# Row sums and their spread by 32x32 block turns and one folding matmul, in an encoder layer with attention and a matrix memory

## The chip, the cores and the metric

One Trainium2 chip, one core. The time is device microseconds of one execution of the whole program; the kernel before takes 2061.98 us (median of three runs, 2061.67 to 2063.15). Lower is better. The engines are TensorE (PE, with PEld for its weight loads), VectorE (DVE), ScalarE (ACT), GpSimd (POOL) and SyncE (SP, which here issues most of the transfers).

## The reference, cut to what matters

One layer is applied to two sequences of 512 tokens with 1024 channels (`x_prompt` and `x_sample`, called 0 and 1 in the kernel), all in float32:

```python
def rms_norm(x, g):
    return x * rsqrt(mean(x * x, axis=-1) + EPS) * g

def mlstm_bidirectional(...):            # 4 heads of 128 channels
    h = h_fwd + h_bwd
    h = h * rsqrt(mean(h * h, axis=-1) + EPS)      # over a head's 128 channels
    return sigmoid(o_pre) * h * head_norm

def encoder_layer(x, ...):
    x = x + 0.5 * swiglu(rms_norm(x, ffn1_norm), ...)        # 1024 -> 2816 -> 1024
    proj = rms_norm(x, mix_norm) @ w_in
    ...                                  # att: 8 query heads, 2 key heads; mem: mlstm_bidirectional
    merged = sigmoid(g_att) * (att @ w_up_att) + sigmoid(g_mlstm) * (mem @ w_up_mlstm)
    x = x + merged @ w_out
    return x + 0.5 * swiglu(rms_norm(x, ffn2_norm), ...)     # then the final rms_norm
```

What the change touches are three of these norms: the one ahead of `w_in` ("mid norm"), the one ahead of the second feed-forward, and the one over each memory head. Each needs, for every token, the sum of squares over the channels, one over its square root, and that number multiplied into every channel.

## The kernel before, in words

**Layout.** The channels lie on the 128 partitions and the 512 tokens along the free dimension, so one tile is 128x512 and a sequence is eight such tiles. A sum over channels is therefore a sum across partitions, and the factor for a token must stand on all 128 partitions. Matmuls are done in parts: an operand is split into a high and a low part, and one product takes three matmuls of 128x128 by 128x512.

**Stages.** The first feed-forward runs over both sequences at once by a scheme of seven products (0 to 640 us of the span). Then come, for sequence 0, its projections (640 to 690), attention (690 to 840), the four memory heads (840 to 945), and the gates together with the projections of sequence 1 (945 to 1075). Sequence 1 has its attention at 1075 to 1225, its memory heads at 1225 to 1330, its merge and output until 1420. The second feed-forward fills 1420 to 2059. The two mixers are generators (`mix`) that are advanced in turns.

**The norm before.** For each tile of squares summed over the channel tiles (`accs`, `acc2`, tag `R`), `stats` takes four steps. `col_sums` turns the 128x512 tile by four TensorE transposes into PSUM (L202), so that tokens lie on partitions, and VectorE sums each 128 (L204) to a 128x4 tile: four columns of 128 tokens. `rstd_cols` computes the inverse root by a shift and three Newton rounds, twelve small VectorE operations (L161, L170, L172, three times L188, L189, L191). `bcast_psum` turns each column, spread over 128, back by four more transposes (L212), and `bcast_cols` copies PSUM to an SBUF tile with the tag `R` (L218). The 128x4 tile is kept as `r[s]` in the mid norms, where it scales values with tokens on partitions. The memory heads do the same on one tile of squares (`h2`, L1238) and let VectorE read PSUM directly when it multiplies (L1244).

**Where they stand.** There are twelve such norms: the mid norm of sequence 0 (`mid_stats(0, 100, 140)`, near 642 us), the mid norm of sequence 1 within the attention of mixer 0 (`mid_parts(1)`), the norm of sequence 0 ahead of the second feed-forward within the attention of mixer 1 (`parts2(0)`), that of sequence 1 at the second feed-forward's start (`stats2(1)`, near 1417 us), and the eight memory heads. The first norm, ahead of the first feed-forward, and the final norm do it in ways of their own and use `col_sums` and `bcast_psum` too; those calls stay.

**What sets the order.** The kernel is written in a tile framework that orders each engine's instructions by priority. Code stands in order of priority as written; `shifted(n)` moves a block later by `n` places, and `pin` keeps an instruction where the program has it. In attention, `extra` is a list of parts that are called at the third key block of heads 2, 3 and so on. Between the heads of the memory stand products of other units (`merge_att`, `out_gate`, `mem_qk`, L789) as filling. In `mem_out`, five rounds alternate four transposes of a 128x512 tile with the twelve matmuls of the head's output (L1235), and then the norm follows; the next head's `mem_head` has its score products (L1185) and their VectorE products (L1201, L1213, L1215).

**Buffers.** `T2` hands out 128x512 tiles from rings by tag: `t2` has 11 buffers, `f2` four, `R` two. PSUM has banks by pool: three for `MM`, one for `PO`, two each for `PS` and `PT`.

## Time and profile before

| | before |
|---|---|
| median of three runs | 2061.98 us (2061.67 to 2063.15) |
| span of the profiled execution | 2059.1 us |
| TensorE busy | 2047.3 us, 99%, 9445 matmuls and transposes |
| TensorE weight loads | 1691.3 us, 82% |
| VectorE busy | 1553.0 us, 75%, 2764 instructions |
| ScalarE busy | 913.0 us, 44%, 1667 instructions |
| GpSimd busy | 92.8 us, 5%, 108 instructions |
| TensorE clock | nine tenths or more in all 40 slices |
| moved to and from memory | 457.97 MB, 222 GB/s on the mean |

The profiled execution is one of its own; its span (2059.1 us) lies 2.9 us under the median of the timed runs, and the profile gives no further time for it. Rows of the profile name the line of the code (L202), the engine, the operation, the tile written and the tiles read (`pst<-ident,t`), the shape, and the count. In rows of the timeline the two numbers ahead are the start and the length in microseconds; what stands in brackets is the wait ahead of a row and what ended it. PSUM tiles are called `mm`, `pso`, `pss` and `pst` after the pools `MM`, `PO`, `PS` and `PT`.

### The profile page before, as it was taken

How to read it: one execution, taken by the hardware profiler on the slowest of the kernel's cores; microseconds unless marked ns; L12 is line 12 of the kernel's file. 1: busy time of each engine (PE TensorE's matmuls, PEld its weight loads, DVE VectorE, ACT ScalarE, POOL GpSimd, SP SyncE). 2: the span in 40 equal slices, each digit the busy share in tenths (PEclk: the TensorE clock that was granted, in tenths of full speed). 3: DMA queues.
4: the chain of work that ended last, by engine and by line, in shares of the span. 5: the costliest groups of instructions: out<-in, count | busy, mean ns of one | idle time of the engine just before them, and what ended most of it. 6: DMA issues, size and time to landing. Idle time of an engine off the chain costs nothing.

```text
span 2059.1 us, 27038 instructions
## 1 busy us (share of the span) xinstructions
PE 2047.3 (99%) x9445; PEld 1691.3 (82%) x9445; DVE 1553.0 (75%) x2764; ACT 913.0 (44%) x1667; POOL 92.8 (5%) x108
## 2 busy tenths in 40 slices
PE   9999999999999999999999999999999999999998
PEld 7888888888888888888888888888888888888887
DVE  8888889886797787675566756455788888796797
ACT  7544444442235567563334553324544444443224
POOL 0000000001003000100120000001000000000001
PEclk9999999999999999999999999999999999999999
DMA  9656556799766753877684345677656555599753
GB/s 321 198 170 221 177 191 205 243 349 348 260 227 247 223 187 130 278 259 242 197 310 160 109 140 200 196 265 239 202 175 202 194 174 184 186 342 347 276 202 119
DMA packets 311015, 457.97 MB, mean 222 GB/s; under 512 B 20232, under 2 KB 182112, under 8 KB 309600
## 3 DMA queue, kind: packets, MB, share of 16 engines
q1 hardware_dynamic: 308800, 450.27, 64.6%
q0 software_dynamic: 1920, 5.72, 0.9%
q8 instruction: 74, 1.21, 0.2%
q14 instruction: 61, 0.50, 0.1%
q10 hardware_dynamic: 160, 0.27, 0.0%
HBM read 288.25 MB, written 167.94 MB: 222 GB/s over the span
## 4 chain that ended last, share of the span: by engine, by line
PE 97%; DVE 1%; ACT 1%; DMA 1%; issue 0%; SPq 0%; ACTq 0%; DVEq 0%
PE mm L789 15%; PE pso L332 12%; PE pst L332 12%; PE mm L332 10%; PE mm L590 8%; PE pss L332 6%; PE mm L776 6%; PE pst L590 4%; PE pss L590 4%; PE mm L756 4%; PE pso L590 3%; PE pso L1066 1%; PE pss L1039 1%; PE pst L1055 1%; PE pso L1235 1%; PE pss L1185 1%
## 5 line engine op out<-in xcount | busy, mean ns | idle before, releaser
L332 PE MATMUL pst<-xc,w 128*128 128x512 f32 x1056 | 253.6, 389 | 0.0
L332 PEld LDWEIGHTS pst<-xc,w 128*128 128x128 f32 x1056 | 198.3, 188 | 41.1
L332 PE MATMUL mm<-xc,w 128*128 128x512 f32 x972 | 229.9, 390 | 0.2 <-ACT f L340 0.2
L332 PEld LDWEIGHTS mm<-xc,w 128*128 128x128 f32 x972 | 181.9, 188 | 38.1 <-ACT f L340 0.6
L590 PE MATMUL mm<-rt,w 128*128 128x512 f32 x765 | 178.9, 389 | 0.0
L789 PE MATMUL mm<-xh,w 128*128 128x512 f32 x560 | 177.6, 393 | 0.0
L590 PEld LDWEIGHTS mm<-rt,w 128*128 128x128 f32 x765 | 143.6, 188 | 29.8
L290 ACT ACTIVATE w<-t 128x512 fp32r<-128x512 f32 x176 | 106.5, 627 | 135.7 <-issue 63.1
L291 DVE TENSOR_TENSOR w<-t,w 128x512 fp32r<-128x512 f32 x176 | 117.8, 688 | 47.9 <-ACT w L290 46.6
L332 PE MATMUL pss<-xc,w 128*128 128x512 f32 x528 | 126.8, 389 | 0.0
L332 PE MATMUL pso<-xc,w 128*128 128x512 f32 x528 | 126.8, 389 | 0.0
L332 PE MATMUL pso<-xc,f 128*128 128x512 f32 x528 | 126.8, 389 | 0.0
L789 PEld LDWEIGHTS mm<-xh,w 128*128 128x128 f32 x560 | 104.7, 188 | 21.2 <-DVE w L239 0.2
L332 PEld LDWEIGHTS pss<-xc,w 128*128 128x128 f32 x528 | 99.2, 188 | 20.5
L332 PEld LDWEIGHTS pso<-xc,w 128*128 128x128 f32 x528 | 99.1, 188 | 20.5
L332 PEld LDWEIGHTS pso<-xc,f 128*128 128x128 f32 x528 | 99.1, 188 | 20.5
L776 PE MATMUL mm<-xh,w 128*128 128x512 f32 x336 | 114.5, 401 | 0.0
L789 PE MATMUL mm<-xl,w 128*128 128x512 f32 x280 | 109.7, 392 | 0.0
L673 ACT ACTIVATE w<-wr 128x512 fp32r<-128x512 f32 x72 | 45.1, 632 | 137.0 <-PE pso L590 71.4
L673 ACT ACTIVATE w<-t 128x512 fp32r<-128x512 f32 x82 | 51.8, 632 | 107.4 <-PE pst L590 62.4
L590 PE MATMUL pst<-rt,w 128*128 128x512 f32 x396 | 93.7, 389 | 0.0
L590 PE MATMUL pss<-rt,w 128*128 128x512 f32 x396 | 93.7, 389 | 0.0
(407 smaller groups left out, 4037.5 us busy)
## 6 DMA issues: line engine op xcount, KB each, us to landing
rt<-rbuf SPq DMA_DIRECT2D x154, 512.0 KB, 5.7
wpark<-w SPq DMA_DIRECT2D x104, 512.0 KB, 3.4
w<-wpark SPq DMA_DIRECT2D x104, 512.0 KB, 4.8
wr<-in_ffn_w_gate_dram SPq DMA_DIRECT2D x62, 512.0 KB, 5.3
rbuf<-tab SPq DMA_DIRECT2D x102, 256.0 KB, 3.9
wr<-in_ffn_w_up_dram SPq DMA_DIRECT2D x44, 512.0 KB, 4.5
rbuf<-f SPq DMA_DIRECT2D x72, 256.0 KB, 4.1
wr<-in_w_in_dram SPq DMA_DIRECT2D x36, 512.0 KB, 5.7
```

Source lines behind the costliest of these rows:

```text
L290: pin(nc.scalar.activation(t[:, 0], src, AF.Copy))
L291: pin(V_.tensor_tensor(t[:, 1], src, f(t[:, 0]), op=ALU.subtract))
L332: nc.tensor.matmul(p, a[:, k, :], xt[:, b, k, :], start=(first and k == 0 and i == 0), stop=(k == HK_ - 1 and i == 2), skip_group_check=True)
L590: nc.tensor.matmul(p, u[:, a, d * P:(d + 1) * P], r[:, b, ts], start=(first and q == 0 and k == 0), stop=(q == len(us) - 1 and k == 2), sk ...
L673: nc.scalar.activation(hi, src, AF.Copy)
L756: nc.tensor.matmul(p[b][:, :N], a[:, k, bs], w_[:, kl, :], start=(k == 0 and i == 0), stop=(k == KD - 1 and i == 2))
L776: pin(nc.tensor.matmul(p[0], a[:, k, :], b, start=(k == 0 and i == 0), stop=(k == n - 1 and i == 2)))
L789: nc.tensor.matmul(p, a[:, k, :], b, start=(k == 0 and i == 0), stop=(k == n - 1 and i == 2))
L1039: pin(nc.tensor.matmul(p, qT[:, h, b * P:(b + 1) * P], kv[:, hk * 2 + j, :], start=(j == 0), stop=(j == 1)))
L1055: pin(nc.tensor.transpose(p[:, b * P:(b + 1) * P], Ps[b][:, kb * P:(kb + 1) * P], ident))
L1066: pin(nc.tensor.matmul(pos[h], Vst[:, kb, h // 4, :], w, start=(kb == 0 and i == 0), stop=(kb == 3 and i == 1)))
L1185: nc.tensor.matmul(p, qk[a][:, isl], qk[b], start=(n == 0), stop=(n == 2))
```

## The change

All twelve norms get their sums and their spread in another way. The four steps become:

- `block_sums`: VectorE turns the tile of squares in blocks of 32x32 (`nc.vector.transpose`) into an `f2` tile, and sums each group of 32 along the free dimension into 16 columns of a tile `row`. Partition 32a + i then holds, in column n, the sum over the 32 channels of group a for token 32n + i.
- `block_rstd`: one TensorE matmul with the constant `fold` (128x128, 1 where the two partitions agree modulo 32) adds the four channel groups and leaves the whole sum on each of them. The twelve small VectorE operations follow, on 16 columns and in place within `row`.
- `spread_rows`: a second block turn of VectorE reads each of the 16 columns 32 times and writes the 128x512 tile of factors to SBUF (tag `R` for the norms, `f2` in the heads), where before it stood in PSUM.
- `row_cols`: for the mid norms alone, four small GpSimd copies make the 128x4 tile `r[s]` from the 16 columns.

`fold` is made by four GpSimd operations in `mix_consts`. In attention the norm is now in three parts, at heads 2, 3 and 4, instead of two, at heads 2 and 3, with the folding matmul pinned. In the memory heads `block_rstd` is shifted by 60 and the spread by 160; before, only the part from `bcast_psum` on was shifted, by 160. One other tile (`et`) shares a buffer (`fa`), and `cs` has one buffer instead of two.

```diff
-    def stats(acc):
-        return rstd_cols(col_sums(acc), 4, D)
-    def bcast_cols(r):
-        pr = bcast_psum(r)
-        R = T2(F32, "R")
-        nc.vector.tensor_copy(R, pr)
+    fold = cpool.tile([P, P], F32, name="fold")
+    def fold_const():
+        part_ = fold[:, 0:32]
+        for a in range(1, 4):
+            src = ident[:, 0:32] if a == 1 else part_
+            nc.gpsimd.tensor_tensor(part_, src, ident[:, a * 32:(a + 1) * 32], op=ALU.add)
+        nc.gpsimd.tensor_copy(fold[:, 32:P].rearrange("p (a j) -> p a j", j=32),
+                              part_.unsqueeze(1).to_broadcast([P, 3, 32]))
+    def block_sums(t, tag="f2"):
+        row = spool.tile([P, 64], F32, tag="row", bufs=1, name=nm("row"))
+        q = T2(F32, tag)
+        nc.vector.transpose(q, t)
+        nc.vector.tensor_reduce(row[:, 0:16], q.rearrange("p (n j) -> p n j", j=32), axis=AX.X, op=ALU.add)
+        return row
+    def block_rstd(row, n, keep=lambda i: i):
+        p = PT()
+        keep(nc.tensor.matmul(p[:, 0:16], fold, row[:, 0:16], start=True, stop=True))
+        V = nc.vector
+        a, y, u = [row[:, 16 * i:16 * i + 16] for i in (1, 2, 3)]
+        V.tensor_scalar(a, p[:, 0:16], 1.0 / n, EPS, op0=ALU.mult, op1=ALU.add)
...
+        return y
+    def row_stats(acc):
+        return block_rstd(block_sums(acc), D)
+    def row_cols(r16):
+        c = spool.tile([P, 4], F32, tag="rc4", bufs=2, name=nm("rc"))
+        for a in range(4):
+            ps_ = slice(a * 32, (a + 1) * 32)
+            nc.gpsimd.tensor_copy(c[ps_, :], r16[ps_, :].rearrange("p (b a) -> p a b", a=4)[:, a, :])
+        return c
+    def spread_rows(r16, R):
+        nc.vector.transpose(R.rearrange("p (n j) -> p n j", j=32), r16.unsqueeze(2).to_broadcast([P, 16, 32]))
         return R
...
-                if extra and b == 2 and h in (2, 3):
+                if extra and b == 2 and h in (2, 3, 4):
                     extra[h - 2]()
...
-            rh = rstd_cols(col_sums(h2), 4, DM)
+            row = block_sums(h2)
+            with shifted(60):
+                rh = block_rstd(row, DM)
             with shifted(160):
-                Rh = bcast_psum(rh)
+                Rh = spread_rows(rh, T2(F32, "f2"))
                 V_.scalar_tensor_tensor(og, og, hn[:, h:h + 1], Rh, op0=ALU.mult, op1=ALU.mult)
                 split(og, mem[:, h, 0, :], mem[:, h, 1, :])
...
     def mid_stats(s, a=0, b=0):
         with shifted(a):
-            r[s] = stats(accs[s])
+            r16 = row_stats(accs[s])
         with shifted(b):
-            R[s] = bcast_cols(r[s])
+            R[s] = spread_rows(r16, T2(F32, "R"))
+            r[s] = row_cols(r16)
...
     def mid_parts(s):
+        got = []
         def one():
-            r[s] = stats(accs[s])
+            got.append(block_sums(accs[s]))
         def two():
-            R[s] = bcast_cols(r[s])
-        return one, two
+            got.append(block_rstd(got[0], D, pin))
+        def three():
+            R[s] = spread_rows(got[1], T2(F32, "R"))
+            r[s] = row_cols(got[1])
+        return one, two, three
...
     def stats2(s):
-        r[s] = stats(acc2[s])
-        R2[s] = bcast_cols(r[s])
+        R2[s] = spread_rows(row_stats(acc2[s]), T2(F32, "R"))
```

`parts2` changes as `mid_parts` does, without `r[s]`. In the changed file the folding matmul is L232, the first block turn L225, its sum L226, the second block turn L258, and the lines of the memory heads lie 41 to 43 further down (L1235 is L1276, L1240 is L1281, L1185 is L1226, L1201 is L1242, and the products of L789 are L830).

TensorE at the third memory head of mixer 0, before: from the last matmuls into the head's output (L1235) over the transposes of the squares (L202) to the next head's scores (L1185), with filling (L789):

```order
L1235 MATMUL pso_7885<-t_931_7913,Vm_7266 128x512
L1235 MATMUL pso_7885<-t_933_7924,Vm_7266 128x512 x2
L1235 MATMUL pso_7885<-t_934_7925,Vm_7266 128x512
L789 MATMUL mm_8168<-att_5939,w_8060 128x512 x4
L202 MATMUL pst_7937<-ident,t_935_7934 128x128 x4
L789 MATMUL mm_8168<-att_5939,w_8060 128x512 x4
L789 MATMUL mm_8192<-att_5939,w_8060 128x512 x4
L1185 MATMUL pss_8018<-qk_7758 128x512 x3
```

The same place now, with the folding matmul (L232) in the place of the transposes:

```order
L1276 MATMUL pso_7844<-t_899_7872,Vm_7251 128x512
L1276 MATMUL pso_7844<-t_901_7883,Vm_7251 128x512 x2
L1276 MATMUL pso_7844<-t_902_7884,Vm_7251 128x512
L830 MATMUL mm_8012<-att_5934,w_7824 128x512 x2
L830 MATMUL mm_8101<-att_5934,w_8006 128x512 x12
L830 MATMUL mm_8125<-att_5934,w_8006 128x512 x2
L232 MATMUL pst_7900<-row_7896,fold 128x16
L830 MATMUL mm_8125<-att_5934,w_8006 128x512 x2
L1226 MATMUL pss_7964<-qk_7717 128x512 x3
```

Between the head's last output matmul and the first norm step on TensorE stood 4 filling matmuls; now there are 16, and the four spreading transposes (L212), which stood 15 rows further on, are gone.

VectorE at the same head, before: after the gating of the head's output (L1240), the sum of the turned squares (L204) and the small operations of the root stand among the products of the next head's scores (L1201):

```order
L1240 SCALAR_TENSOR_TENSOR box_5279<-box_5279,pso_7885 128x512
L1201 SCALAR_TENSOR_TENSOR t_951_7996,dn_7991<-pss_7992,t_951_7996 128x128
L204 TENSOR_REDUCE cs_7942<-pst_7937 128x4
L1201 SCALAR_TENSOR_TENSOR t_952_7999,dn_7991<-pss_7992,t_952_7999 128x512
L161 TENSOR_SCALAR rs_7944<-cs_7942 128x4
L1201 SCALAR_TENSOR_TENSOR t_954_8009,dn_7991<-pss_8005,t_954_8009 128x256
L170 TENSOR_SCALAR rs_7946<-rs_7944 128x4
```

And now:

```order
L1281 SCALAR_TENSOR_TENSOR box_5274<-box_5274,pso_7844 128x512
L225 STREAM_TRANSPOSE f_905_7897<-t_903_7893 128x512
L1242 SCALAR_TENSOR_TENSOR t_911_7942,dn_7937<-pss_7938,t_911_7942 128x128
L226 TENSOR_REDUCE row_7896<-f_905_7897 128x16
L1242 SCALAR_TENSOR_TENSOR t_912_7945,dn_7937<-pss_7938,t_912_7945 128x512
L1242 SCALAR_TENSOR_TENSOR t_914_7955,dn_7937<-pss_7951,t_914_7955 128x256
L1242 SCALAR_TENSOR_TENSOR t_915_7959,dn_7937<-pss_7951,t_915_7959 128x384
L1242 SCALAR_TENSOR_TENSOR t_917_7968,dn_7937<-pss_7964,t_917_7968 128x384
L235 TENSOR_SCALAR row_7896<-pst_7900 128x16
```

The block turn stands right behind the gating and ahead of the next head's products; the small operations moved behind five of those products. The spreading turn (L258) comes after the last scaling of the next head's tiles, and the multiplication with it (L1287, before L1244) two rows later.

TensorE at the start of the second feed-forward, where sequence 1's norm stands among the first products (L332), before:

```order
L332 MATMUL mm_12495<-xc_12013,w_12492 128x512 x12
L332 MATMUL mm_12555<-xc_12013,w_12547 128x512 x2
L202 MATMUL pst_12510<-ident,R_12226 128x128 x4
L332 MATMUL mm_12555<-xc_12013,w_12547 128x512 x10
L332 MATMUL mm_12495<-xc_12014,w_12492 128x512 x3
L212 MATMUL pst_12538<-ident,rs_12536 128x128 x4
L332 MATMUL mm_12495<-xc_12014,w_12492 128x512 x9
```

And now (L332 is L372):

```order
L372 MATMUL mm_12361<-xc_11879,w_12358 128x512 x12
L372 MATMUL mm_12406<-xc_11879,w_12398 128x512 x8
L232 MATMUL pst_12380<-row_12376,fold 128x16
L372 MATMUL mm_12406<-xc_11879,w_12398 128x512 x4
L372 MATMUL mm_12361<-xc_11880,w_12358 128x512 x12
```

The fold stands six products later than the transposes did, and nothing of the norm is left on TensorE behind it. Of the transfers, the first four loads from `xbuf` for the next sequence's projections (L1591) and the first four from `x2buf` (L1617) stand later in SyncE's queue than before, at place 567 instead of 544 and 717 instead of 705; both go into `f2` tiles, of which each head now takes two more.

20 lines of the change are left out of this document (15 added, 5 removed).

## Prediction

> **What bounds the kernel now.** I read the page's busy times and its chain first, then what TensorE itself waited for.
>
> ```profile
> span 2059.1 us, 27038 instructions
> PE 2047.3 (99%) x9445; PEld 1691.3 (82%) x9445; DVE 1553.0 (75%) x2764; ACT 913.0 (44%) x1667; POOL 92.8 (5%) x108
> PEclk9999999999999999999999999999999999999999
> PE 97%; DVE 1%; ACT 1%; DMA 1%; issue 0%; SPq 0%; ACTq 0%; DVEq 0%
> PE pst L987 <- DVE t L674: 0.7, 2, 0.5
> PE pst L212 <- DVE rs L191: 0.2, 1, 0.2
> ```
>
> TensorE is busy 99% of the span, at the full clock in every slice, and it carries 97% of the chain that ended last. The last two rows are from the list of TensorE's waits: between the start-up and the end it waits for almost nothing. So the end is set by how long TensorE's own instructions take in their order. A microsecond taken from that order comes off the end, as long as no other engine becomes late. VectorE, at 75%, is where the change puts its work.
>
> By stage, the table of windows has the attention of the first mixer (690 to 840), its memory heads (840 to 945), and the same two stages of the second mixer (1075 to 1225, 1225 to 1330):
>
> ```profile
> 690.00:840.00 150.00, 149.77 (x746) 122.27 (x745) 121.19 (x246) 103.26 (x205) 1.58 (x1) 1.00 0.58 190
> 840.00:945.00 105.00, 105.00 (x497) 84.78 (x496) 73.46 (x194) 54.93 (x118) 6.68 (x5) 1.00 0.78 255
> 1225.00:1330.00 105.00, 105.00 (x500) 85.66 (x499) 60.56 (x182) 40.57 (x101) 0.00 (x0) 1.00 0.57 187
> ```
>
> The columns after the length are busy time and count of PE, PEld, DVE and ACT. VectorE has 32 us of 105 free in the first memory and 44 in the second.
>
> **What leaves TensorE.** The replaced steps are four norms (two mid norms, two before the second feed-forward) and eight memory heads. Each had four transposes that turned the squares (L202) and four that spread the result (L212): 12 x 8 = 96.
>
> ```profile
> L202 PE MATMUL pst<-ident,t x32: 271/273/275, 843.1 to 1307.9; 128*128 128x128 f32 x32
> L202 PE MATMUL pst<-ident,R x20: 270/272/328, 641.5 to 2035.2; 128*128 128x128 f32 x20
> L212 PE MATMUL pst<-ident,rs x48: 270/272/323, 648.0 to 1421.5; 128*128 128x128 f32 x48
> ```
>
> Of the 20 in the second row, four belong to the final norm of the first sequence, which stays; 32 + 16 + 48 = 96. A duration of 272 ns isn't the price, since matmuls overlap. The price is read from starts, in the timeline of TensorE at the first head, against the rhythm of plain matmuls from the chain in order of time:
>
> ```profile
> 1421.81 48.30 PE mm L332 x213
> 842.18 1.07 PE L789 MATMUL mm<-att,w 128*128 128x512 f32 x4
> 843.09 0.60 PE L202 MATMUL pst<-ident,t 128*128 128x128 f32 x4
> 843.44 0.47 PE L789 MATMUL mm<-xh,w 128*128 128x512 f32 x1
> 843.76 0.39 PE L789 MATMUL mm<-xl,w 128*128 128x512 f32 x1
> ```
>
> 48.30 / 213 = 0.227 us per matmul. From the first transpose to the second matmul behind the four it is 843.76 - 843.09 = 0.67 us, of which one matmul is 0.227; the four cost 0.44, or 0.111 each. 96 x 0.111 = 10.7 us.
>
> The Trainium skill ("TensorE: Matmul & The Clock Gate", Part 4: PE-mode transpose) gives about 390 ns for a 128x128 transpose in isolation and about 275 ns in one kernel. The trace agrees with 275 as the duration of one (272), but by this sum the path holds only 0.111 of it; whoever summed durations would get 96 x 0.272 = 26.1 us, which is a rival below.
>
> **What enters TensorE.** Twelve matmuls with the 128x128 `fold` and 16 columns, in full float32. The gates already have six of that shape in each mixer:
>
> ```profile
> 680.76 0.51 PE L919 MATMUL pst<-Lt,tab 128*128 128x16 f32 x4
> 681.12 0.37 PE L919 MATMUL pst<-Lt,ones 128*128 128x16 f32 x2
> 681.35 0.60 PE L919 MATMUL pst<-Lt,tab 128*128 128x16 f32 x4
> 681.79 0.37 PE L919 MATMUL pst<-Lt,ones 128*128 128x16 f32 x2
> 682.02 0.49 PE L789 MATMUL mm<-xh,w 128*128 128x512 f32 x1
> 682.34 0.40 PE L789 MATMUL mm<-xl,w 128*128 128x512 f32 x1
> ```
>
> Six in the code are twelve in the trace, so each makes two passes. 682.34 - 680.76 - 0.227 = 1.35 us for twelve, 0.113 a pass, 0.226 a matmul: 12 x 0.226 = 2.7 us. TensorE's own balance is -10.7 + 2.7 = **-8.0 us**.
>
> **What VectorE does instead.** Per step it adds a turn of 128x512 in 32x32 blocks, a sum over 16 groups of 32, and a turn that spreads 16 columns to 512. It drops the sum of the transposed squares and, in the four norms, a copy from PSUM. The twelve little operations stay, on 16 columns instead of 4.
>
> ```profile
> L204 DVE TENSOR_REDUCE cs<-pst x13: 680/691/693, 642.6 to 2035.5; 128x4 f32<-128x512 f32 x13
> L218 DVE COPY R<-pst x4: 683/691/692, 649.2 to 1422.1; 128x512 f32<-128x512 f32 x4
> L188 DVE SCALAR_TENSOR_TENSOR rs<-rs x48: 152/163/194, 644.0 to 1420.6; 128x4 f32<-128x4 f32 x36, 128x8 f32<-128x8 f32 x6, 128x32 f32<-128x32 f32 x6
> L929 DVE TENSOR_TENSOR_SCAN f<-f x2: 402/406/411, 684.4 to 1039.9; 32x128 f32<-32x128 f32 x2
> ```
>
> The little ones hardly change: their extremes are 152 and 194 ns, with 4 and 32 columns among the forms. The sum is as long as the old one. No row shows a block turn. Its nearest is the copy of the same 128x512, 0.69 us, and I take that. A turn below it, down to half, would gain nothing, since TensorE is then simply served earlier. The upper end is VectorE's slowest kind per column, the scan: about 0.4 us for 128 columns against about 0.15 of fixed cost, so 0.25 / 128 x 512 + 0.15 = 1.2 us. Together 24 turns less 4 copies are 20 x 0.69 = 14 us in a VectorE with 500 us free over the span, and nothing on the path unless TensorE stands waiting.
>
> The Trainium skill ("VectorE: DVE Perf Modes", The three transpose paths) gives 311 ns for a block turn of 128x128 in bf16 on VectorE; no run here shows one yet, and an estimate from it lies near my 0.69. Its Rules for kernel authors send a 128x128 transpose to TensorE where PSUM will do. By that rule this change would be worth nothing; by the rows TensorE is the full engine, and the sum goes by the rows.
>
> **The new wait.** TensorE now waits at the folding matmul for the row of sums, and every matmul queued behind it waits too. The chain is read at the first head:
>
> ```profile
> 841.16 1.18 PE L1235 MATMUL pso<-t,Vm 128*128 128x512 f32 x4
> 842.38 0.60 ACT L1238 ACTIVATE t<-pso 128x512 f32<-128x512 f32 x1 [2.16 <-PE pso L1235]
> 843.01 0.69 DVE L1240 SCALAR_TENSOR_TENSOR box<-box,pso 128x512 f32<-128x512 f32 x1 [1.30 <-ACT t L1238]
> 843.61 0.68 DVE L1151 SCALAR_TENSOR_TENSOR mg<-mg,mm 128x512 f32<-128x512 f32 x1
> ```
>
> The last matmul into the head's PSUM ends at 842.34; ScalarE squares until 842.98; VectorE starts L1240 at 843.01 and can start the next thing at 843.61. Turn 0.6 and sum 0.69 then end at about 844.9, which is 2.6 us after that matmul, or 2.8 to 3.2 with one other operation between them. The order of the changed kernel has 24, 15, 16 and 13 matmuls between the last such matmul and the fold in the first memory, 31, 19, 13 and 13 in the second. At 0.227 less the 0.16 by which the last one ends after its successor's start, that is 5.3, 3.2, 3.5, 2.8 and 6.9, 4.2, 2.8, 2.8 us. Needed are 3.2, 3.2, 2.9, 2.6 and 3.2, 2.6, 2.9, 2.6. The margins are 2.1, 0, 0.6, 0.2 and 3.7, 1.6, -0.1, 0.2: with 0.69 us per turn the waits sum to about 0.1 us, with 1.2 us to about 1.7.
>
> In the norm before the second feed-forward's last part the old chain made TensorE wait, and the new one is as tight:
>
> ```profile
> 1416.60 0.69 DVE L155 TENSOR_TENSOR R<-R,t 128x512 f32<-128x512 f32 x1
> 1417.34 0.66 PE L202 MATMUL pst<-ident,R 128*128 128x128 f32 x4
> 1417.75 3.23 PE L332 MATMUL mm<-xc,w 128*128 128x512 f32 x13
> 1421.16 0.65 PE L212 MATMUL pst<-ident,rs 128*128 128x128 f32 x4 [0.18 <-DVE rs L191]
> ```
>
> The fold stands six matmuls behind the place of the old transposes, 1417.34 + 1.36 = 1418.7; the row is there at 1417.29 + 0.6 + 0.69 = 1418.6. The wait of L212 goes with L212: -0.2. Within attention the three parts stand a head, some 13 us, apart, and hide; if they didn't, one part would cost about 1 us, twice.
>
> **What else moves.** The four copies on GpSimd per mid norm have a small copy as their row below, 4 x 0.18 = 0.7 us; the first reader of these scales comes about ten microseconds later, so nothing. Two more buffers per head from the ring `f2` make the early loads for the next stage (L1591, L1617) stand later in SP's queue, ahead of weights:
>
> ```profile
> L907 POOL COPY Fs<-gt x8: 180/184/189, 660.9 to 1001.6; 128x4 f32<-128x4 f32 x8
> 946.19 0.45 SPq L231 DMA_DIRECT2D wr<-in_w_up_mlstm_dram  x1
> 973.49 2.88 PE L789 MATMUL pst<-mem,w 128*128 128x512 f32 x12
> ```
>
> The last of these weights are issued at 946.2 and the fourth product with them starts at 973.5, so a few microseconds in that queue are covered; uncovered they would cost as much as they are late. Order among the other matmuls of the heads shifts too. There the ten matmuls of a head's output run with less filling between them, and VectorE's two splits behind them can be late by a fraction of their 0.69. I allow 0.1 us per head, 0.8 in all, with bounds of -0.5 (some of today's tiny waits close) and 3.6 (0.45 per head).
>
> Sum: -10.7 + 2.7 - 0.2 + 0.1 + 0.8 = **-7.3 us**. The profiled span would be 2059.1 - 7.3 = 2051.8; the median of the runs lies 2.9 above the span, for what is around it, so 2061.98 - 7.3 = **2054.7 us**.
>
> **Rivals.**
> 1. *The gain goes into waits at the fold.* Turns near 1.2 us cost 1.7 in the heads, 0.5 at the last norm, and in-order VectorE then hands the next head's tiles over late, up to 0.5 in six gaps: 2.2 + 3 = 5.2 instead of 0.9. Result -8.2 + 5.2 = -3.0, 2059 us. For it: four of eight margins are 0.2 or less. Against: all 128x512 rows are near 0.69.
> 2. *Slower: the turn is a slow instruction.* At 3 us a turn, 2.3 more than assumed, the eight margins leave 0.2, 2.3, 1.7, 2.1 and 0, 0.7, 2.4, 2.1, with the last norm 2.2, in all 13.7 of waiting: -8.2 + 13.7 = +5.5, 2067.5 us. It decides from about 2.2 us a turn on, where the waits reach 8. Against: no VectorE row with 512 columns comes near.
> 3. *The filling matters.* The re-laid order of the heads loses 0.45 per head, as in the bound: -8.1 + 3.6 = -4.5, 2057.5 us. For it: TensorE's order in the heads was full. Against: its matmuls are nearly the same ones, two or three places off.
> 4. *Durations count.* If each transpose held TensorE for its 0.272 us, the balance would be -26.1 + 2.7 = -23.4, 2038.6 us. The starts above speak against it.
>
> **Chances.** The forecast (a gain of 5.5 to 9) has 0.64, rival 1 0.15, rival 2 0.05, rival 3 0.13, rival 4 0.03. About 0.2%, 4.1 us, is what a measurement of this kernel can tell from no change, so faster means under 2057.9. The forecast, rival 4, three quarters of rival 3 and a small part of rival 1 lie there: 0.79. The rest of 1 and 3 lie within: 0.15; slower, 0.06. The range runs from 2052.3 (all waits gone and today's tiny ones with them: -8.2 - 0.5, and 1 us for the rounding of 0.111) to 2059, rival 1.
>
> **What would show it.** Right: 96 fewer transposes and 24 more passes of 16 columns, group cost as above; block turns near 0.69; list of TensorE's waits without new rows above 0.5 us; TensorE's busy time down by 8. Wrong: turns of a microsecond or more with fold waits behind them, or waits of L1227 and L1235 in the heads grown by over 3 us in all.

## The result and the profile after

The changed kernel takes 2054.39 us (median of four runs, 2052.86 to 2055.41) beside 2062.36 for the kernel before (four runs, 2061.67 to 2063.15): a ratio of 0.9960, with a 95% interval of 0.9948 to 0.9972. That is 8.0 us less. A second series of five runs gave 2054.77 beside 2063.24, ratio 0.9963 (0.9950 to 0.9975). The forecast was 2054.7, within 2052.3 to 2059.0.

The page of the changed kernel:

```profile
span 2053.4 us, 26928 instructions
PE 2040.7 (99%) x9373; PEld 1685.7 (82%) x9373; DVE 1569.9 (76%) x2784; ACT 914.5 (45%) x1667; POOL 95.0 (5%) x120
PE 96%; DMA 2%; DVE 1%; ACT 1%; issue 0%; SPq 0%; ACTq 0%; DVEq 0%
```

TensorE has 72 instructions fewer (96 transposes gone, 24 passes of the fold come) and 6.6 us less busy time; VectorE has 16.9 us more. TensorE is still the bound. The profiled execution itself moved less than the medians, 2059.1 to 2053.4, and the one of the changed kernel was the slowest of its four (2055.41; a span lies about 2.0 below the time of the same execution). Where the rest comes from is read by landmarks in TensorE's timeline: the first scores of the first attention, the first product of the second feed-forward, and the last group of all, in the kernel before:

```profile
709.64 0.39 PE L1039 MATMUL pss<-kv,qT 128*128 128x512 f32 x1
...
1414.16 2.20 PE L332 MATMUL mm<-xc,w 128*128 128x512 f32 x9
...
2051.12 1.24 PE L606 MATMUL mm<-w,rt 128*128 128x256 f32 x9
```

And after, where each line lies some 40 further down:

```profile
711.00 0.39 PE L1080 MATMUL pss<-kv,qT 128*128 128x512 f32 x1
...
1408.42 1.75 PE L372 MATMUL mm<-xc,w 128*128 128x512 f32 x7
...
2044.53 1.24 PE L646 MATMUL mm<-w,rt 128*128 128x256 f32 x9
```

From the first landmark to the last it is 1341.48 us before and 1333.53 after: 7.95 less, with eleven of the twelve norms in between. In the second profiled execution of the changed kernel, from its second series, the same stretch took 1333.60 (710.30 to 2043.90), so this measure came out the same to 0.1. The changed execution was 1.36 late at the first landmark, though one norm had already been made cheaper, and its end lay 0.9 further behind its last group (2053.4 - 2044.53 against 2059.1 - 2051.12). The late start begins with a wait in the first feed-forward, which the change doesn't touch. TensorE and then VectorE of the changed kernel show it:

```profile
44.01 1.88 PE L372 MATMUL mm<-xc,w 128*128 128x512 f32 x7 [0.90 <-DVE t L1539]
```

```profile
43.27 0.69 DVE L1539 TENSOR_TENSOR t<-t,mm 128x512 f32<-128x512 f32 x1 [1.17 <-DMA kept<-t]
```

VectorE waited 1.17 us for a write to memory to be done, and TensorE waited behind it. GpSimd had issued this write of `kept`, and it took 5.2 us from issue to landing, where it took 3.3 in the kernel before. In the profiled executions of all these kernels, whose code is the same there, the last product of that feed-forward's first half (L332 before) started anywhere from 435.8 to 439.1 us. So the stretch between the first and the last landmark is the fairer measure of one execution, and the medians are that of the whole.

**The new instructions.** The rows of the block turns in the heads (L225, L258), of the sum (L226) and of the fold (L232) in the changed kernel, with minimum, median and maximum in ns:

```profile
L225 DVE STREAM_TRANSPOSE f<-t x8: 703/704/706, 844.0 to 1302.5; 128x512 f32<-128x512 f32 x8
L258 DVE STREAM_TRANSPOSE f<-row x8: 704/711/712, 853.6 to 1307.5; 128x512 f32<-128x512 f32 x8
L226 DVE TENSOR_REDUCE row<-f x12: 665/685/687, 637.9 to 1412.3; 128x16 f32<-128x512 f32 x12
L232 PE MATMUL pst<-row,fold x24: 177/262/283, 643.8 to 1413.2; 128*128 128x16 f32 x24
```

By its medians a block turn takes 0.704 to 0.711 us, 2 to 3% above the 0.69 of the copy that the prediction took for it. The 24 rows of the fold are twelve matmuls in two passes.

**Its place in TensorE's order.** The first head's fold, with nothing to wait for, and the second head's, from TensorE's timeline in the changed kernel:

```profile
847.73 0.39 PE L830 MATMUL mm<-xl,w 128*128 128x512 f32 x1
847.96 0.29 PE L232 MATMUL pst<-row,fold 128*128 128x16 f32 x2
848.10 0.71 PE L830 MATMUL mm<-xh,w 128*128 128x512 f32 x2
848.64 0.40 PE L830 MATMUL mm<-xl,w 128*128 128x512 f32 x1
...
879.73 0.61 PE L830 MATMUL mm<-xh,w 128*128 128x512 f32 x2
880.23 0.37 PE L232 MATMUL pst<-row,fold 128*128 128x16 f32 x2
880.44 0.47 PE L830 MATMUL mm<-xl,w 128*128 128x512 f32 x1
880.76 0.63 PE L830 MATMUL mm<-xh,w 128*128 128x512 f32 x2
```

At the first head 847.73 to 848.64 holds three matmuls and the fold: 0.91 - 3 x 0.227 = 0.23 us, the price that was expected. At the second, 879.73 to 880.76 holds three matmuls and the fold: 1.03 - 0.68 = 0.35, so 0.12 of it is waiting. Read in this way at all twelve places, the folds take 3.58 us; 2.75 is their own price, and 0.83 is waiting at five of them (0.12, 0.14, 0.21, 0.14 in heads and 0.22 at the start of the second feed-forward). None of it shows in the list of TensorE's waits, which has no row of L232. The list has one new row above 0.5 us, the 0.9 of the first feed-forward shown above.

VectorE at the first head, for the chain that leads to the fold:

```profile
843.35 0.69 DVE L1281 SCALAR_TENSOR_TENSOR box<-box,pso 128x512 f32<-128x512 f32 x1 [1.51 <-ACT t L1279]
843.95 0.70 DVE L225 STREAM_TRANSPOSE f<-t 128x512 f32<-128x512 f32 x1
844.58 0.65 DVE L1192 SCALAR_TENSOR_TENSOR mg<-mg,mm 128x512 f32<-128x512 f32 x1
845.15 0.67 DVE L226 TENSOR_REDUCE row<-f 128x16 f32<-128x512 f32 x1
```

The sum is done at 845.82 and the fold starts at 847.96: 2.1 us of margin, as the prediction had worked out for this head.

### The profile page after: what moved, and what is told of

It is laid out like the page before. It is cut to its first block, busy times and chain, and to the rows that moved or that the text cites. A ratio compares the mean times of both kernels' runs of the same rounds, so it can differ in the third digit from the quotient of the medians.

```text
span 2053.4 us, 26928 instructions
## 1 busy us (share of the span) xinstructions
PE 2040.7 (99%) x9373; PEld 1685.7 (82%) x9373; DVE 1569.9 (76%) x2784; ACT 914.5 (45%) x1667; POOL 95.0 (5%) x120
## 4 chain that ended last, share of the span: by engine, by line
PE 96%; DMA 2%; DVE 1%; ACT 1%; issue 0%; SPq 0%; ACTq 0%; DVEq 0%
PE mm L830 15%; PE pso L372 12%; PE pst L372 11%; PE mm L372 10%; PE mm L630 8%; PE pss L372 6%; PE mm L817 6%; PE pst L630 4%; PE pss L630 4%; PE mm L797 4%; PE pso L630 3%; PE pso L1107 1%; PE pss L1080 1%; PE pst L1096 1%; PE pso L1276 1%; PE pss L1226 1%
## 5 line engine op out<-in xcount | busy, mean ns | idle before, releaser
L372 PE MATMUL pst<-xc,w 128*128 128x512 f32 x1056 | 253.8, 389 | 0.0
L372 PEld LDWEIGHTS pst<-xc,w 128*128 128x128 f32 x1056 | 198.2, 188 | 41.4 <-ACT t L407 0.3
L372 PE MATMUL mm<-xc,w 128*128 128x512 f32 x972 | 229.7, 390 | 1.2 <-DVE t L1539 0.9
L372 PEld LDWEIGHTS mm<-xc,w 128*128 128x128 f32 x972 | 181.9, 188 | 39.3 <-DVE t L1539 1.1
L830 PE MATMUL mm<-xh,w 128*128 128x512 f32 x560 | 176.8, 392 | 0.0
L372 PE MATMUL pso<-xc,f 128*128 128x512 f32 x528 | 127.0, 389 | 0.2 <-DVE t L411 0.2
L372 PE MATMUL pss<-xc,w 128*128 128x512 f32 x528 | 126.8, 389 | 0.0
L372 PE MATMUL pso<-xc,w 128*128 128x512 f32 x528 | 126.8, 389 | 0.0
L830 PEld LDWEIGHTS mm<-xh,w 128*128 128x128 f32 x560 | 104.9, 188 | 21.2
L372 PEld LDWEIGHTS pso<-xc,f 128*128 128x128 f32 x528 | 99.0, 188 | 21.2 <-DVE t L411 0.6
L372 PEld LDWEIGHTS pss<-xc,w 128*128 128x128 f32 x528 | 99.1, 188 | 20.6
L372 PEld LDWEIGHTS pso<-xc,w 128*128 128x128 f32 x528 | 99.1, 188 | 20.6
L830 PE MATMUL mm<-xl,w 128*128 128x512 f32 x280 | 109.5, 391 | 0.0
```

The lines of the kernel that those rows point to most:

```text
L372: nc.tensor.matmul(p, a[:, k, :], xt[:, b, k, :], start=(first and k == 0 and i == 0), stop=(k == HK_ - 1 and i == 2), skip_group_check=True)
L830: nc.tensor.matmul(p, a[:, k, :], b, start=(k == 0 and i == 0), stop=(k == n - 1 and i == 2))
```

## The experiments

All times are medians beside runs of the kernel before on the same chip. The changed kernel is 2054.39 or, in its second series, 2054.77. The median of the kernel before moved between 2062.36 and 2063.24 from series to series, so a difference between two kernels of different series is uncertain by some 0.9. Where it matters, the stretch between the two landmarks is given beside the medians, from one profiled execution each.

**The two halves.** First the heads alone with the new way, the norms as before:

```diff
-            r16 = row_stats(accs[s])
+            r[s] = stats(accs[s])
...
-            R[s] = spread_rows(r16, T2(F32, "R"))
-            r[s] = row_cols(r16)
+            R[s] = bcast_cols(r[s])
```

(and the same in the other three norms, in two parts within attention).

> The eight memory heads use block turns and the fold as in the changed kernel; the four norms keep their transposes as before. Theory A (a step is worth what its matmuls take from TensorE's order): the four norms lose 4.35 us of transposes (their places in the trace of before: 1.97 for the squares, 2.4 for the spread) and gain 1.15 us of folds, so this kernel stands 3.2 us above the changed kernel and 4.8 below the one before: about 2057.6. Rival (the gain comes from the shorter chain of one place alone, the last norm at the second feed-forward's start or the heads): 0 or 8 of the 8 us remain.

Measured: 2057.18 beside 2062.68, ratio 0.9972 (0.9960 to 0.9983): 5.5 less than before, 2.8 above the changed kernel.

Then the norms alone:

```diff
-            row = block_sums(h2)
-            with shifted(60):
-                rh = block_rstd(row, DM)
+            rh = rstd_cols(col_sums(h2), 4, DM)
             with shifted(160):
-                Rh = spread_rows(rh, T2(F32, "f2"))
+                Rh = bcast_psum(rh)
```

> The four norms use block turns and the fold in three parts as in the changed kernel; the eight memory heads keep their transposes. Theory A: the heads lose 7.9 us of transposes and gain 2.4 us of folds and their waits, so this kernel stands 5.4 us above the changed kernel and 3.2 below the one before: about 2059.2; the two halves add up to the whole within 1 us. Rival (re-ordering in the heads, not the transposes, brought part of the gain or cost part of it): the sum of the two halves misses the whole by more than 1 us.

Measured: 2059.60 beside 2062.68, ratio 0.9984 (0.9976 to 0.9993): 3.1 less than before. The halves give 5.5 + 3.1 = 8.6, the whole 8.0 to 8.5: they add up within the scatter, and each is worth about what its transposes less its folds take from TensorE. Read place by place once more, the transposes of the four norms take 4.1 us and those of the heads 7.6, not the 4.35 and 7.9 of the two expectations. Less the folds and their waits that makes 2.9 us above the changed kernel for the heads alone and 5.1 for the norms alone; measured are 2.8 and 5.2.

**The price of a transpose.** Six transposes that nobody reads, in front of each head's fold:

```diff
         p = PT()
+        if extra is not None:
+            for b in (1, 2, 3) * 2:
+                bs = slice(b * P, (b + 1) * P)
+                nc.tensor.transpose(p[:, bs], extra[:, bs], ident)
...
-                rh = block_rstd(row, DM)
+                rh = block_rstd(row, DM, extra=h2)
```

> The changed kernel with six transposes of 128x128 put in front of the fold at each of the eight heads, 48 in all; they turn the head's squares into PSUM columns that nothing reads. Theory A (price by starts): 48 x 0.111 = 5.3 us more than the changed kernel, less up to 0.5 us of waits at the folds that they fill: 2059.2 to 2059.7. Rival (price by durations, 0.272 each): 13.1 us more, 2067.5. Third (TensorE has room at these places): no change.

Measured: 2060.02 beside 2062.68 (ratio 0.9985, 0.9976 to 0.9994), 5.6 more than the changed kernel: 0.117 each. (In the stretch it is 6.1 more, 0.127 each.) That kernel's row of these transposes, and TensorE at its first head:

```profile
L235 PE MATMUL pst<-ident,t x48: 270/272/275, 847.0 to 1308.3; 128*128 128x128 f32 x48
```

```profile
847.00 0.48 PE L834 MATMUL mm<-xh,w 128*128 128x512 f32 x1
847.32 0.27 PE L235 MATMUL pst<-ident,t 128*128 128x128 f32 x1
847.34 0.48 PE L834 MATMUL mm<-xh,w 128*128 128x512 f32 x1
847.66 0.27 PE L235 MATMUL pst<-ident,t 128*128 128x128 f32 x1
847.68 0.48 PE L834 MATMUL mm<-xl,w 128*128 128x512 f32 x1
```

Each lasts 0.272 by its own row, and yet a matmul and a transpose together take 847.34 - 847.00 = 0.34 us, 0.11 more than the matmul alone. The price by durations would have made 13.1 us; it is refuted.

**The cost on VectorE.** The block turn of the squares three times over, into the same tile:

```diff
-        nc.vector.transpose(q, t)
+        for _ in range(turns):
+            nc.vector.transpose(q, t)
...
-            row = block_sums(h2)
+            row = block_sums(h2, turns=3)
```

> The changed kernel with the block turn of each head's squares done three times over instead of once, so VectorE has 16 more turns of 0.704 us, 11.3 us, ahead of the sums. In the order the fold stands 11, 10, 17, 10 and 8 matmuls later at five of the eight heads. Theory A (VectorE's time counts only where TensorE waits for it): waits at the folds stay below 0.5 in all, and the time moves by less than 1.5 us. Rival B (VectorE in the heads is as good as on the path: what stands behind the turns, the next head's tiles, comes 1.4 us late at each of eight heads): 5 to 11 us more, with waits of the transposes and matmuls of the next head in TensorE's list.

Measured: 2054.57 beside 2062.68 (ratio 0.9956, 0.9943 to 0.9970), 0.2 from the changed kernel. VectorE's timeline of that kernel at the second head:

```profile
879.27 0.70 DVE L226 STREAM_TRANSPOSE f<-t 128x512 f32<-128x512 f32 x1
879.90 0.65 DVE L1016 TENSOR_TENSOR box<-mm,R 128x512 f32<-128x512 f32 x1
880.47 0.69 DVE L226 STREAM_TRANSPOSE f<-t 128x512 f32<-128x512 f32 x1
881.09 1.21 DVE L280 TENSOR_TENSOR w<-wr,w 128x1024 fp32r<-128x1024 f32 x1
882.21 0.70 DVE L226 STREAM_TRANSPOSE f<-t 128x512 f32<-128x512 f32 x1
882.95 0.69 DVE L227 TENSOR_REDUCE row<-f 128x16 f32<-128x512 f32 x1
```

The sum ends 4.37 us after the first turn's start (883.64 - 879.27), where it took 1.87 with one turn; TensorE had eleven more matmuls, 2.5 us, ahead of its fold. The order is not fixed: the framework lays it out anew, and the fold goes to where its row is expected to be ready. So a chain made longer by turns that the framework counts moves the fold, and TensorE has other matmuls for the time. A turn that took longer on the chip than the framework expects would meet the order as it stands, and no run tests that.

Then the limit, seven turns (`turns=7`):

> The changed kernel with the block turn of each head's squares done seven times over, so VectorE has 48 more turns, 33.8 us, 17 of them in each memory, where it had 23 us of 105 free in the first and 39 in the second. In the order the folds stand 3 to 35 matmuls later than in the changed kernel, at seven of the eight heads by enough for the 4.2 us. Theory A (the order follows the chain, VectorE has room): within 1.5 us of the changed kernel. Rival B (the next head's tiles come late, VectorE full in the first memory): 3 to 15 us more, with waits in TensorE's list at the heads' transposes and output matmuls. With the step as the prediction had it, fixed places and a turn of 4.9 us, the waits would be 25 us or more.

Measured: 2058.27 beside 2062.59 (ratio 0.9980, 0.9971 to 0.9989), 3.9 more than the changed kernel; and the same 48 more turns put behind the fold instead,

```diff
-                Rh = spread_rows(rh, T2(F32, "f2"))
+                Rh = T2(F32, "f2")
+                for _ in range(7):
+                    spread_rows(rh, Rh)
```

> The changed kernel with the spreading turn of each head done seven times over into the same tile, so VectorE has the same 48 more turns as in the run with seven turns ahead, but behind the fold and the root, where only the multiplication of the head's output waits. Theory A (the 3.8 us lost there came from tiles of the next head that stood behind the turns): less lost than there, 0 to 2 us more than the changed kernel. Rival B (VectorE is simply full in the first memory, wherever the turns stand): 3 us or more, again in the first memory's heads.

Measured: 2058.35 beside 2062.60 (ratio 0.9979, 0.9970 to 0.9988), 4.0 more, with the widest scatter of all kernels (2055.57 to 2060.24). The first memory of the changed kernel, of the seven turns ahead, and of the seven behind, from the table of windows (busy time of PE, PEld and VectorE after the length):

```profile
840.00:945.00 105.00, 105.00 (x486) 85.61 (x485) 81.82 (x203) 55.76 (x118) 6.43 (x5) 1.00 0.76 250
```

```profile
840.00:945.00 105.00, 102.97 (x466) 82.95 (x466) 93.10 (x215) 54.10 (x115) 6.91 (x5) 0.98 0.73 235
```

```profile
840.00:945.00 105.00, 104.79 (x484) 85.06 (x484) 92.84 (x224) 55.19 (x116) 6.06 (x5) 1.00 0.76 250
```

VectorE is busy 93 of 105 us in both. TensorE's lists of waits name the same tiles in both, those of the next head's products, first with the turns ahead, then behind:

```profile
PE pss L1227 <- DVE t L1243: 1.8, 1, 1.8
```

```profile
PE pss L1226 <- DVE t L1242: 2.8, 2, 2.6
```

They don't stand at the same place, though. With the turns ahead the wait is in the first memory, and in the matmuls behind it TensorE's granted clock (the third number from the end) fell to 0.53:

```profile
895.19 1.40 PE L1227 MATMUL pss<-qk 128*128 128x512 f32 x3 [1.81 <-DVE t L1243]
895.30:898.70 3.40, 3.40 (x9) 2.68 (x10) 2.54 (x10) 0.37 (x1) 0.00 (x0) 0.53 0.81 199
```

3.40 us at 0.53 of the clock cost about 1.6 us, nearly as much as the wait itself; the two make 3.4 of the 5.7 us that this execution is longer in the stretch. With the turns behind, it is 3.6 us longer. The first memory then has a wait of only 0.2 us, and the long one is in the second memory, where VectorE is busy 81 of 105 us. The seven turns (L258) stand there ahead of the next head's products (L1242) in VectorE's order, TensorE waits for these, and its clock stays full:

```profile
1225.00:1330.00 105.00, 102.38 (x473) 83.05 (x472) 81.18 (x213) 38.04 (x91) 0.00 (x0) 1.00 0.62 190
1233.73 2.95 DVE L258 STREAM_TRANSPOSE f<-row 128x512 f32<-128x512 f32 x4
1242.51 0.28 DVE L1242 SCALAR_TENSOR_TENSOR t<-pss,t 128x128 f32<-128x128 f32 x1
1243.47 0.73 PE L1226 MATMUL pss<-qk,qk 128*128 128x512 f32 x2 [2.62 <-DVE t L1242]
```

So the loss is as large with the turns before the fold as behind it, as rival B said, and theory A falls in both by its size. But that VectorE is full in the first memory doesn't explain it: at 93 of 105 us there the second run waited 0.2, and at 81 of 105 in the second memory 2.6. In both profiled executions most of the loss is at one head, at which the next head's products came late in VectorE's order. Why at that head is not shown, and the other executions may have lost their time elsewhere.

**Is the third part needed?** Fold and root right behind the sums in attention:

```diff
         def one():
             got.append(block_sums(accs[s]))
+            got.append(block_rstd(got[0], D, pin))
 
         def two():
-            got.append(block_rstd(got[0], D, pin))
+            pass
```

> The changed kernel with the norm in attention in two parts a head apart: the fold and the root stand right behind the sums in the first part, the spread in the third. Theory A: TensorE waits at the fold for the turn and the sum, 1.4 us from the turn's start to the sum's end in the first attention and 2.9 in the second in the trace of the changed kernel, less a few matmuls: 2 to 4 us more, 2056.5 to 2058.5, with two rows of the fold in TensorE's list of waits. Rival (other matmuls of attention fill in front of the fold): no change.

Measured: 2054.31 beside 2062.59 (ratio 0.9965, 0.9952 to 0.9977): no change. VectorE and then TensorE of that kernel in the first attention:

```profile
752.42 0.69 DVE L226 TENSOR_REDUCE row<-f 128x16 f32<-128x512 f32 x1
```

```profile
755.97 0.29 PE L232 MATMUL pst<-row,fold 128*128 128x16 f32 x2
```

The sum ends at 753.11, the fold starts 2.9 us later. Other matmuls of attention stand ahead of it, and the third part is worth nothing that these runs can show. Theory A of this run falls.

**Without the fold.** VectorE adds the four partition groups itself:

```diff
-        p = PT()
-        keep(nc.tensor.matmul(p[:, 0:16], fold, row[:, 0:16], start=True, stop=True))
         V = nc.vector
+        c = row[:, 0:16]
         a, y, u = [row[:, 16 * i:16 * i + 16] for i in (1, 2, 3)]
+        for w in (64, 32):
+            for lo in range(0, P, 2 * w):
+                V.tensor_copy(u[lo:lo + w, :], c[lo + w:lo + 2 * w, :])
+                V.tensor_copy(u[lo + w:lo + 2 * w, :], c[lo:lo + w, :])
+            V.tensor_tensor(c, c, u, op=ALU.add)
-        V.tensor_scalar(a, p[:, 0:16], 1.0 / n, EPS, op0=ALU.mult, op1=ALU.add)
+        V.tensor_scalar(a, c, 1.0 / n, EPS, op0=ALU.mult, op1=ALU.add)
```

> The changed kernel without the folding matmul: VectorE adds the four groups of 32 partitions itself, by six small copies to other partitions and two small additions on 16 columns, at all twelve places. Theory A: TensorE loses 12 folds with their waits, 3.6 us by their places in the trace of the changed kernel; VectorE has 96 more small operations of about 0.16 us, 15 us, behind nothing that TensorE waits for soon: 2051 us, 3 to 4 below the changed kernel. Rival (the longer chain of VectorE, 1.3 us per step, comes late where the spread is needed, above all at the start of the second feed-forward): no gain, or up to 3 us more than the changed kernel, with waits of the products on the normed tiles.

Measured: 2053.52 beside 2062.59 (ratio 0.9959, 0.9945 to 0.9972). That is 0.9 below the changed kernel, within the scatter, where 3.6 had been expected. TensorE's waits in that kernel between 640 and 1420 us:

```profile
PE pst L1032 <- DVE t L718: 1.9, 3, 1.1
PE pst L1272 <- DVE row L244: 0.4, 1, 0.4
PE pst L1272 <- DVE t L1258: 0.4, 1, 0.4
```

In the changed kernel this stretch has one row:

```profile
PE pst L1028 <- DVE t L714: 0.8, 2, 0.6
```

L1272 are the transposes of the next head's tiles; one of them now stands waiting behind VectorE's work on `row`. The largest of the new waits, the 1.1 in the first row, belongs to no norm. ScalarE and then VectorE waited there for a weight that landed late and that they split, and TensorE waited behind them, ahead of the attention of sequence 1:

```profile
1050.46 1.06 ACT L282 ACTIVATE w<-wr 128x1024 fp32r<-128x1024 f32 x1 [0.91 <-DMA wr<-in_w_out_dram]
1051.56 1.22 DVE L283 TENSOR_TENSOR w<-wr,w 128x1024 fp32r<-128x1024 f32 x1 [1.09 <-ACT w L282]
1053.27 0.96 PE L1032 MATMUL pst<-ident,t 128*128 128x128 f32 x7 [1.10 <-DVE t L718]
```

The same with GpSimd in VectorE's place for the eight operations (`nc.gpsimd.tensor_copy` and `nc.gpsimd.tensor_tensor`):

> As in the run without the folding matmul, but the six copies between partitions and the two additions are done by GpSimd, idle 95% of the time, so VectorE gets nothing new. Theory A' (the run without the fold gained only 0.9 us instead of 3.5 because VectorE's 96 small operations pushed other work late): TensorE loses the folds' 3.6 us and nothing comes late in the heads: 2050.5 to 2052. Rival (the longer chain itself, whoever does it, comes late where the spread is needed; on GpSimd it is longer still, 8 x 0.18 us and two hand-overs): 2053 to 2056. Second rival (the loss there was a weight load that came late, of its own accord): also about 2051, but with no difference in the waits of the heads from the VectorE form.

Measured: 2054.49 beside 2062.60 (ratio 0.9963, 0.9949 to 0.9976): no gain, though VectorE gets no new work. The waits at the next heads' transposes are there again (0.4 and 0.3 us), and so is the one behind the weight (0.9). In the stretch the two kernels took 1334.14 and 1334.36 us, 0.6 and 0.8 more than the changed kernel. The rival of both runs was right in the time. Its cause, the longer chain, shows in part of the waits; the weight that comes late, the second rival of this run, shows in the other part, though not in a time of about 2051.

Two runs took the step apart. First the fold left out, with nothing in its place, so that each norm takes a quarter of its channels:

```diff
-        p = PT()
-        keep(nc.tensor.matmul(p[:, 0:16], fold, row[:, 0:16], start=True, stop=True))
...
-        V.tensor_scalar(a, p[:, 0:16], 1.0 / n, EPS, op0=ALU.mult, op1=ALU.add)
+        V.tensor_scalar(a, row[:, 0:16], 1.0 / n, EPS, op0=ALU.mult, op1=ALU.add)
```

> The changed kernel with the folding matmul left out and nothing in its place: the root is taken of each group of 32 channels' own sum, so the norms are computed over a quarter of the channels. TensorE loses twelve folds and their waits, 3.6 us by their places in the changed kernel's trace, and VectorE gets nothing new. Theory C (in the runs without the fold the gain was lost because the longer chain or the added small operations made TensorE wait elsewhere): the 3.6 us appear here, 2050.5 to 2051.5. Rival D (in these places another engine sets the pace, so a microsecond less on TensorE is worth less than one): 0 to 2 us, 2052.5 to 2054.5, with longer waits of TensorE for VectorE's tiles.

Measured: 2051.34 beside 2063.24 (ratio 0.9943, 0.9930 to 0.9957), 3.4 below the changed kernel beside it (2054.77), with single runs from 2049.33 to 2053.05. In the stretch it is 2.3 less, 1331.27 us for eleven of the folds: the wait behind the weight is here too, with 0.6, though no chain is longer, and there is a new one of 0.3 at a head. Then the fold kept, with the eight small operations added behind the first step of the root:

```diff
         V.tensor_scalar(a, p[:, 0:16], 1.0 / n, EPS, op0=ALU.mult, op1=ALU.add)
+        for w in (64, 32):
+            for lo in range(0, P, 2 * w):
+                V.tensor_copy(u[lo:lo + w, :], a[lo + w:lo + 2 * w, :])
+                V.tensor_copy(u[lo + w:lo + 2 * w, :], a[lo:lo + w, :])
+            V.tensor_tensor(y, a, u, op=ALU.add)
```

> The changed kernel with the fold kept and eight small VectorE operations put behind it at each of the twelve places (six copies between partitions and two additions into columns that are overwritten), the same 96 as in the run without the fold. Theory C: they cost 2 to 3 us, what that run lost. Rival D: 0 to 1 us, since nothing waits for these operations soon.

Measured: 2056.68 beside 2063.24 (ratio 0.9970, 0.9958 to 0.9981), 1.9 above the changed kernel. In the stretch it is 1.7 more, 1335.26. So leaving out the twelve folds brought 3.4 us by the medians, near the 3.6 of their prices and waits, and less by the stretch. The 96 small operations cost 1.9, though they are only 15 us of VectorE's time and nobody reads their results. But the other steps of the root stand behind them: from the first step to the last the root takes 1 to 2.5 us longer at eleven of the twelve places, so this run has the longer chain too and doesn't part it from VectorE's added work. In the run without the fold, 3.4 less 1.9 is 1.5; 0.9 was measured, which the scatter allows. Theory C holds by the medians: the fold's time appears when nothing takes its place, and the longer chain with its operations takes back more than half of it. Which of TensorE's matmuls lose the 1.9 isn't settled: this kernel's list of waits between 640 and 1420 has only one new row, of 0.2 us, so the loss is spread over waits below what the list shows.

The changed kernel beside these two:

> The changed kernel once more beside the two above, for a comparison on the same chip: 2054.4, within 1 us, by every theory. The 8 us below the kernel before should show again with a narrower interval, and the waits at the five folds should be the same five.

Measured: 2054.77, as told at the top, and the waits at the folds are the same five, 0.84 us in all.

## Why the prediction was right, point by point

- **What bounds the kernel** was right: TensorE at 99% before and after, and the time follows TensorE's own work. The extra transposes (5.6 us more) and the fold left out (3.4 less) show it from both sides.
- **The transposes, -10.7.** The rule was right, starts and not durations. The size was a little low. Read place by place in the trace of before as the prediction read one head, the 96 took 11.6 us, 0.4 of it the wait at the last norm (0.2 in the prediction). Groups of four stand at 0.44 to 0.46, and transposes standing singly among matmuls at 0.11 to 0.12 each; but the spread ahead of the next head's scores took 0.59 to 0.60 at three heads.
- **The folds, +2.7** came out at 2.75 for the work.
- **The fold's waits, +0.1** were mis-sized: 0.83. The margins were right in order: at the two first heads, with 2.1 and 3.7, there was no wait, and the five places that waited are those with margins of 0.2 or less. But a fold that waited started 0.05 to 0.15 us after the sum's end and not at it. A margin of 0.1 or 0.2 is therefore no margin, and the prediction had taken the hand-over from VectorE to TensorE as nothing.
- **The order of the heads, +0.8** was the other miss: TensorE's places make -11.64 + 3.58 = -8.1, and 8.0 to 8.5 less was measured in the medians, so nothing is left for it. (For the eleven norms of the stretch the places make 7.4 and the stretch 7.95; where the other 0.6 comes from is not traced.) The bound's middle was a guess, and its value is about zero. So the gain was put 0.7 too low at the transposes, 0.7 too high at the waits and 0.8 too low at the order. That the first two cancel is luck; the third is what parts the forecast of 7.3 from the measured 8.0 to 8.5.
- **From span to median, 2.9.** A span lies about 2.0 below the time of the same execution (2053.4 and 2055.41); the other 0.9 was an execution faster than the median. It cancels in the forecast, which starts from the median.
- **The signs.** Of those named for being right, the counts and the turns near 0.69 came. TensorE's busy time fell by 6.6 over the whole execution and not by 8; in the stretch between the landmarks it fell by 7.7 (1340.46 to 1332.75). The one new wait above 0.5 us is that of the first feed-forward.
- **VectorE's 14 us hide** (16.9 by the page), right: two more turns per head, 11.3 us, changed the time by 0.2. The rule of the Trainium skill ("VectorE: DVE Perf Modes", Rules for kernel authors) that a 128x128 transpose goes to TensorE where PSUM will do didn't decide here, where the change does without a 128x128 transpose: with TensorE at 99% and VectorE at 75%, twelve norms by block turns and a fold took 8.0 us less. Its other line there, that 32x32 turns are fastest on VectorE, no run here tests.
- **The rival on the slower side**, a slow turn, fell with the turns' 0.704 to 0.711 us. Its "in all 13.7 of waiting" came from margins in a fixed order, and that step holds only for a slowness that the framework doesn't count on, which no run tests. With three turns for one, 1.4 us more of turns per head, the order followed the chain and nothing happened. With seven, 3.9 us were lost; in the profiled execution 1.8 went into a wait at one head and some 1.6 into a lower clock behind it.
- **Three parts a head apart**: that one part "would cost about 1 us, twice", if they didn't stand apart, was wrong; with the fold in the first part nothing changed. The pinned fold still had attention's matmuls ahead of it.
- **Durations count** was wrong as a rival, by the 48 transposes: 5.6, not 13.1.
- **The copies on GpSimd and the later loads** were put at nothing. No row shows otherwise: TensorE waited for neither in the changed kernel. No run took them alone.

## What to carry to other kernels

Where one engine is full, price a removed instruction by the distance between starts in its own stage, at every place and not at one, and compare the sum with that of what replaces it; here the sum made afterwards, -8.1, lies within what the medians gave, 8.0 to 8.5 less. Work moved to another engine is free only in so far as nothing behind it in that engine's queue is due: 11 us of turns cost nothing, and 15 us of small operations in the middle of a chain cost 1.9. The busy share of a stage doesn't tell where it will cost. With a framework that orders by readiness, a chain made longer by more instructions moves its consumer before it makes it wait, so margins of the present order say little about such a chain. A change of a few microseconds is read from medians, and in single profiles from a stretch between two landmarks that leaves out what the change doesn't touch.

## What the runs showed of the hardware

- A turn of 128x512 in 32x32 blocks takes VectorE 0.704 to 0.711 us, 2 to 3% longer than a copy of the same tile (0.69), also where its input is 16 columns read 32 times each.
- A float32 matmul pass of 16 columns takes TensorE's order 0.113 us, as long as a transpose of 128 columns (0.111): in these two the width doesn't count. The runs don't show where that ends.
- The last write of the output, from its issue on ScalarE's queue to the end of the span, took 4.1 us before (2055.00 to 2059.1) and 5.0 after (2048.42 to 2053.4), with the same instructions ahead of it. Such differences, and the 1.2 us of a write in the first feed-forward, make the span of one profiled execution a poor measure of a change of 8 us.
- After a wait of 1.81 us, TensorE's granted clock was 0.53 for 3.4 us (seven turns ahead); after a wait of 2.62 us in another kernel it stayed full (seven turns behind). What decides between the two isn't shown.
